# Projections of a pair of heads as one continuous stream over all pairs, shifted by half a period, with one PSUM pool of six banks

## The chip, the cores and the metric

The program runs on one core of one Trainium2 chip. The metric is device time in microseconds (us) for one execution. The engines are named as in the profile: PE (TensorE, matmuls and transposes; PEld are its weight loads), DVE (VectorE), ACT (ScalarE), POOL (GpSimd) and SP (SyncE, here the queue that issues nearly all DMAs). Each engine works through its own queue in order and waits on semaphores for the others.

## The reference, cut to what matters

The reference is a trunk of two layers on a sequence of 1024 positions of width 1024. The change touches only the token mixer of layer 0, the forgetting attention with 16 heads of width 64:

```python
def forgetting_attention(h, w_in, b_f, q_gain, k_gain, w_out):
    proj = h @ w_in                                   # [1024,1024] @ [1024, 4*1024+16]
    q, k, v, o, fl = jnp.split(proj, [D, 2 * D, 3 * D, 4 * D], axis=-1)
    q = rmsnorm(q.reshape(B, S, H, Dh), q_gain)
    k = rmsnorm(k.reshape(B, S, H, Dh), k_gain)
    F = jnp.cumsum(jax.nn.log_sigmoid(fl + b_f), axis=1).transpose(0, 2, 1)
    for qb in range(S // Q_BLOCK):                    # 8 blocks of 128 queries, causal
        logits = einsum('bqhd,bkhd->bhqk', q[:, q0:q1], k[:, :q1]) * Dh ** -0.5
        logits = where(kpos <= qpos, logits + F[:, :, q0:q1, None] - F[:, :, None, :q1], -inf)
        outs.append(einsum('bhqk,bkhd->bqhd', softmax(logits), v[:, :q1]))
    return (concatenate(outs) * sigmoid(o)) @ w_out
```

After it come `x + g1 * y`, a convolutional feed-forward, a spatial-gating layer with its own feed-forward, and a last norm. These later stages take the larger part of the time and the change leaves their code as it is.

## The kernel before, in words

Everything is computed in fp32 precision by splitting each operand into a high and a low part (`pair`: ACT casts the high part, DVE subtracts for the low part) and running three matmuls per product (`mm3`). All of the attention stands in one method, `fox`.

First come the norm of x, the modulation vectors and the gate o. The `o_proj` calls for the last five slices of o are mixed with `run_jobs`: each of its jobs reads 2 MB of `ada_w`, adds it up on DVE (`ada_part`, line 268) and ends in four tiny PE matmuls against a column of ones and one DVE add (line 283). The tiny matmuls, the transposes of q and k, and the transposes of the attention weights all use one PSUM pool of two banks, `ms`, whose users are chained in program order.

Then the heads are worked in eight pairs, p = 0 to 7. A pair needs:

- `proj(p)`: the columns of q, k and v for the pair, 8 blocks of 128 positions, each block 8 steps of three matmuls of 128x384 (192 matmuls named `pj<-x,h` in the profile). It is a generator that yields after each step, 64 steps in all. Its weights come by DMA through two `fraw` buffers and are split into eight `x` buffers (`weights`). After four blocks (a half) the norm of q and k runs on ACT and DVE, into one `qkv` buffer.
- `heads_qk(half)`: eight transposes (`ms<-ident,qkv`), from which ACT and DVE make the scaled high and low parts `qq`, `kh`, `kl`. `heads_v`: the same for v, without PE.
- `scores(qt)`, qt = 0 to 7: matmuls `s<-kh,qq` and `s<-kl,qq` for both heads, up to 512 keys a piece, a DVE pass that subtracts the bias built on POOL and takes the extremum (line 715), then the exponential and the scaling on ACT and DVE.
- `values(g, hd)`, g = 0 to 3: for each block of keys up to four transposes of the weights into an `ms` bank (`ms<-ident,cv` and `ms<-ident,raw`), the split into a `pt` buffer on ACT (line 750) and DVE (line 119), and matmuls with v, `pv<-pt,w`, issued one block later (`later`). At the end of a group the result is gated and written to DRAM (`nat`).

The projections of the next pair are the filler. `tick` takes as many steps from the generator `fill` as work was just issued: `n / P` for a piece of scores, 1 or 2 for a block of values. At the end of a pair `drain` takes what is left. For p = 7 the filler is `out_early`, the first part of the output projection (`pj<-h,h`, 128x512), whose operands come in pieces through the same two `fraw` buffers (`out_piece`); ahead of it `x_transposed` brings x and transposes it (64 transposes `ms<-ident,h`).

PSUM has eight banks: two for `ms`, three for `s` (pool `fs`), two for `pj` (pool `fpj`), one for `pv` (pool `fpv`).

The order on each engine is not the order of the source. A scheduler goes through the program with priorities in the order of the source and puts an instruction ahead when the ones before it are not ready and it has its buffers. With two banks of its own, `pj` can be taken ahead of the source at any place where PE would be without work.

Of the kernel before, what the change touches and what calls it, by code (L numbers as in the profile page):

```python
# [18 lines left out]
P = 128  # L19
# [48 lines left out]
class Trunk:  # L68


    def __init__(self, ctx, tc, **io):
        self.ctx, self.tc, self.nc = ctx, tc, tc.nc
        self.__dict__.update(io)
        self.chains = {}
        self.strict = self.ordered = False
        self.pending = None
        self.hooks = []
        self.ra, self.rx = "a", "X"
        self.n = 0
# [23 lines left out]
    def mm(self, out, lhsT, rhs, start, stop):  # L103
        i = self.nc.tensor.matmul(out, lhsT, rhs, start=start, stop=stop, skip_group_check=self.strict)  # L104
        return self.chain("pe", i) if self.strict else i
# [47 lines left out]
    def transpose4(self, srcs):  # L153

        ps = self.tile(self.ms, [P, 512], F32, "ms")
        for j, s in enumerate(srcs):
            i = self.nc.tensor.transpose(ps[: s.shape[1], j * P : (j + 1) * P], s, self.ident)  # L157
            if j == 0:
                self.chain("ms", i)
# [183 lines left out]
    def fox(self):  # L343
# [9 lines left out]
        with ExitStack() as es:  # L353
# [20 lines left out]
            def ps1(pool, tag):  # L374
                return pool.tile([P, 512], F32, tag=tag, name=self.name(tag))
# [22 lines left out]
            def raw_pieces():  # L398
# [7 lines left out]
                return [T([P, 2, 2, 256], F32, "pt", 2) for _ in range(2)]  # L406
# [65 lines left out]
            for p in range(3):  # L472
                for half in range(2):
                    acc[p, half] = ps1(*((ps_s, "s") if p == 0 else (ps_p, "pj")) if p < 2 else (ps_s, "s") if half else (ps_v, "pv"))
# [28 lines left out]
            def o_out(p, half, ps):  # L503
                t = T([P, 512], F32, "pt", 2)
# [7 lines left out]
            def o_proj(p):  # L512
                w = o_weights(3 * D + p * P)
                ps = [ps1(ps_s, "s"), ps1(ps_p, "pj")]
# [15 lines left out]
            def weights(p):  # L530
                ws = []
                n = 400 if p == 0 else 384
                for k0 in range(0, KT, 2):
                    raw = T([P, 2, 400], F32, "fraw", 2)
                    for t in range(3):
                        i = nc.sync.dma_start(
                            raw[:, :, t * P : (t + 1) * P],
                            w_in[k0 * P : (k0 + 2) * P, t * D + p * P : t * D + (p + 1) * P].rearrange(
                                "(k p) f -> p k f", p=P
                            ),  # L540
# [3 lines left out]
                    if p == 0:  # L544
                        nc.sync.dma_start(
                            raw[:, :, 384:], w_in[k0 * P : (k0 + 2) * P, 4 * D :].rearrange("(k p) f -> p k f", p=P)
                        )
                    for j in range(2):
                        t = self.xslot([P, 2, 400], F32R)
                        ws.append(self.pair(t[:, :, :n], raw[:, j, :n], "x"))  # L550
                return ws

            def proj(p, ws, rw):

                n = 400 if p == 0 else 384
                for half in range(2):
                    r = T([P, 4, 384], F32, "qkv", 3)
                    for s in range(4):
                        ps = ps1(ps_p, "pj")
# [60 lines left out]
            self.fill, self.due = iter(()), 0.0  # L620

            def tick(w):
                self.due += w
                while self.due >= 1:
                    self.due -= 1
                    next(self.fill, None)

            def drain():
                for _ in self.fill:
                    pass  # L630
                self.due = 0.0

# [29 lines left out]
            def heads_v(rw):  # L662
                v = self.wslot([P, NST, 256])
                for half in range(2):
                    vs = rw[half][:, :, 256:384].rearrange("p s (g d) -> p s g d", d=DH)
                    vd = v[:, 4 * half : 4 * half + 4, :].rearrange("p s (g d) -> p s g d", d=DH)
                    i = nc.scalar.copy(vd[:, :, 0:4:3, :], vs)
                    if half == 0:
                        self.chain("w", i)
                    self.split_lo(vd[:, :, 1:3, :], vs, vd[:, :, 0:4:3, :])  # L670
                return v
# [1111 lines left out]
```

## Time and profile before

| | us |
|---|---|
| median of three runs | 2730.57 (2730.3 to 2733.01) |
| the profiled execution | 2729.37 |
| its span | 2727.6 |
| PE busy (share of the span) | 2582.4 (95%) |
| DVE busy | 2092.0 (77%) |
| ACT busy | 1460.2 (54%) |
| POOL busy | 164.5 (6%) |
| first and last start of `s<-kh,qq` | 202.4 and 777.4 |
| first and last start of `pv<-pt,w` | 218.2 and 809.3 |

A row of busy time by stretch gives, for each engine, the microseconds in which it was busy and in brackets the number of instructions, then the mean granted clock of PE as a share of its full clock (PEclk), and the share and rate of the DMAs. A row of a timeline gives the start, the time to the end of the last instruction of the row, the engine, line, operation, what it writes and reads, and the count; idle time before it stands in square brackets with the instruction that ended it. Ends of matmuls are modelled and overlap, so the price of a matmul in a stream is read from one start to the next.

### The profile page before, as it was taken

Reading aid. Unit: us, or ns where it says so; the run is one execution under the profiler, and the core shown is the slowest. Engines: PE = TensorE matmul, PEld = TensorE weight load, DVE = VectorE, ACT = ScalarE, POOL = GpSimd, SP = SyncE. Lnnn points to the kernel's source line nnn. Section 1 sums busy time; section 2 is a strip of 40 time slices with the busy share of each in tenths; the row PEclk is TensorE's granted clock in tenths of the full one; section 3 lists DMA queues with packets and bytes.
Section 4 is the critical chain, followed back from the end, with each engine's and each line's share of the span. In section 5 each row is a group of like instructions: output and inputs, shape, how many; then the busy total and the mean of one; then the engine's idle time right before and its main releaser. Section 6 shows DMA issues by size and latency. Waiting matters only on the chain.

```text
span 2727.6 us, 35317 instructions
## 1 busy us (share of the span) xinstructions
PE 2582.4 (95%) x12522; PEld 2189.0 (80%) x12522; DVE 2092.0 (77%) x3630; ACT 1460.2 (54%) x2310; POOL 164.5 (6%) x289
## 2 busy tenths in 40 slices
PE   6999899998797899999999999999999999999997
PEld 5999888886685788888888878888877788888886
DVE  7467777678786888898688777666788888877875
ACT  7327666667654554454545654554456455545444
POOL 1012222223100000000000000000000000000000
PEclk8999999988897999999999999999999999999999
DMA  6572111131113144554846346557552343337562
GB/s 229 169 241 62 43 51 47 45 110 62 56 55 124 62 132 135 161 159 151 289 152 206 97 136 184 188 183 278 158 173 85 112 143 101 124 101 283 162 198 91
DMA packets 315512, 377.61 MB, mean 138 GB/s; under 512 B 18760, under 2 KB 196040, under 8 KB 315336
## 3 DMA queue, kind: packets, MB, share of 16 engines
q1 hardware_dynamic: 315112, 375.30, 42.1%
q8 instruction: 98, 1.61, 0.2%
q14 instruction: 78, 0.64, 0.1%
q10 hardware_dynamic: 224, 0.06, 0.0%
HBM read 285.57 MB, written 89.72 MB: 138 GB/s over the span
## 4 chain that ended last, share of the span: by engine, by line
PE 82%; DVE 10%; ACT 2%; issue 2%; DMA 2%; SPq 1%; POOL 0%; DVEq 0%; POOLq 0%; ACTq 0%
PE bankX L104 19%; PE banka L104 17%; PE bankY L104 17%; PE pj L104 14%; PE ms L104 5%; PE s L104 3%; PE ms L157 3%; PE pv L104 2%; DVE ow L994 1%; DVE hc L994 1%; DVE x L994 1%; PE ms L1600 1%; DVE x L1479 1%; DVE rw L994 1%; SPq L421 1%
## 5 line engine op out<-in xcount | busy, mean ns | idle before, releaser
L981 ACT CAST ow<-rw 128x1024 fp32r<-128x1024 f32 (+1 forms) x438 | 398.7, 911 | 474.6 <-PE bankX L104 156.3
L994 DVE TENSOR_TENSOR ow<-rw,ow 128x1024 fp32r<-128x1024 f32 (+1 forms) x438 | 457.7, 1046 | 171.9 <-ACT ow L981 171.4
L104 PE MATMUL bankX<-hc,ow 128*128 128x512 f32 x1920 | 470.3, 393 | 17.5 <-DVE ow L994 9.6
L104 PEld LDWEIGHTS bankX<-hc,ow 128*128 128x128 f32 x1920 | 361.0, 189 | 95.4 <-DVE ow L994 11.4
L104 PE MATMUL banka<-hc,ow 128*128 128x512 f32 x1608 | 393.4, 393 | 6.5 <-ACT hc L981 2.8
L104 PE MATMUL bankY<-hc,ow 128*128 128x512 f32 x1584 | 388.6, 392 | 0.8 <-DVE ow L994 0.8
L104 PEld LDWEIGHTS banka<-hc,ow 128*128 128x128 f32 x1608 | 301.1, 189 | 71.3 <-ACT hc L981 4.4
L104 PEld LDWEIGHTS bankY<-hc,ow 128*128 128x128 f32 x1584 | 296.5, 188 | 64.3 <-issue 1.9
L104 PE MATMUL pj<-x,h 128*128 128x384 f32 (+1 forms) x1536 | 302.0, 346 | 6.5 <-ACT qkv L566 6.5
L104 PEld LDWEIGHTS pj<-x,h 128*128 128x128 f32 x1536 | 272.8, 192 | 9.7 <-ACT qkv L566 7.5
L1479 DVE SCALAR_TENSOR_TENSOR x<-x,prm,x 128x1023 f32<-128x1023 f32 (+1 forms) x160 | 204.3, 1279 | 2.7 <-ACT x L1477 2.1
L104 PE MATMUL bankY<-ow 128*128 128x512 f32 x720 | 203.6, 391 | 0.2 <-DVE x L998 0.2
L104 PE MATMUL banka<-ow 128*128 128x512 f32 x672 | 187.3, 391 | 0.5 <-DVE x L998 0.5
L104 PEld LDWEIGHTS bankY<-ow 128*128 128x128 f32 x720 | 135.2, 188 | 28.5 <-DVE x L998 0.6
L104 PE MATMUL bankX<-ow 128*128 128x512 f32 x588 | 156.3, 392 | 0.0
L104 PEld LDWEIGHTS banka<-ow 128*128 128x128 f32 x672 | 125.8, 188 | 27.3 <-ACT x L1028 0.8
L104 PE MATMUL pv<-pt,w 128*128 128x256 f32 (+1 forms) x640 | 124.4, 309 | 18.6 <-DVE pt L119 10.1
L104 PE MATMUL ms<-ow 128*128 128x512 f32 x546 | 139.9, 390 | 0.9 <-DVE pp L994 0.9
L119 DVE TENSOR_TENSOR pt<-ms,pt 128x512 fp32r<-128x512 f32 (+1 forms) x160 | 100.1, 631 | 47.7 <-ACT pt L750 46.6
L104 PEld LDWEIGHTS pv<-pt,w 128*128 128x128 f32 x640 | 103.2, 208 | 33.5 <-DVE pt L119 16.4
L104 PEld LDWEIGHTS bankX<-ow 128*128 128x128 f32 x588 | 110.8, 188 | 23.9 <-issue 1.0
L104 PEld LDWEIGHTS ms<-ow 128*128 128x128 f32 x546 | 102.0, 188 | 23.7 <-DVE pp L994 2.9
(299 smaller groups left out, 3883.5 us busy)
## 6 DMA issues: line engine op xcount, KB each, us to landing
rw<-yd SPq DMA_DIRECT2D x210, 256.0 KB
rw<-in_ffn_w_up_dram SPq DMA_DIRECT2D x88, 512.0 KB
yd<-pp SPq DMA_DIRECT2D x60, 512.0 KB
rw<-in_ada_w_dram SPq DMA_DIRECT2D x48, 512.0 KB
rw<-in_ffn_w_down_dram SPq DMA_DIRECT2D x88, 256.0 KB
rw<-in_sgu_w_in_dram SPq DMA_DIRECT2D x32, 512.0 KB
yd<-x SPq DMA_DIRECT2D x30, 512.0 KB
fraw<-in_fox_w_in_dram SPq DMA_DIRECT2D x96, 128.0 KB
```

Source lines behind the costliest of these rows:

```text
L104: i = self.nc.tensor.matmul(out, lhsT, rhs, start=start, stop=stop, skip_group_check=self.strict)
L119: return (eng or self.nc.vector).tensor_tensor(lo, full, hi.bitcast(F32), op=ALU.subtract)
L157: i = self.nc.tensor.transpose(ps[: s.shape[1], j * P : (j + 1) * P], s, self.ident)
L421: i = nc.sync.dma_start(r[:, :, t, :], src[:, :, t, q * 256 : (q + 1) * 256])
L981: return self.ao(self.nc.scalar.copy(t[:, 0], src))
L994: return self.vo(self.nc.vector.tensor_tensor(out, a, b, op=op))
L1479: stt(o[:, j:], a[:, : S - j], w[2 - j], o[:, j:], op0=ALU.mult, op1=ALU.add)
L1600: k = nc.tensor.matmul(px[:, b * P : (b + 1) * P], vn[:, b, c * P : (c + 1) * P], sg[:, 0], start=True, stop=True)
```

## The change

The attention's projections become one generator over the pairs 1 to 7, `stream`, and not one per pair. It is no longer drained at the end of a pair: `tick` takes 0.85 of a step per unit of work, and `until` only makes sure that the half that is needed next is there. So the projections of pair p run from the middle of pair p - 1 to the beginning of pair p, half 0 before `heads_qk(rws[p], 0)` and half 1 after the first scores of pair p. The weights of the next pair are loaded and split inside the last block of a projection, buffer by buffer as its last readers are done. After the last projection the same stream does the transposes of x and `out_early`.

The three PSUM pools become one of six banks that `s`, `pv`, `pj`, `op` (the output projection) and `o` share. The matmuls with v run two blocks behind the transposes and not one, for which `pt` gets a third buffer. `bns`, a tile of a later stage, moves from one SBUF pool to another. The flag `inorder` is never set to true, so the chains that hang on it are not made.

```diff
-            ps_s = es_p.enter_context(tc.tile_pool(name="fs", bufs=3, space=PSUM, reuse_waits="tile"))
-            ps_p = es_p.enter_context(tc.tile_pool(name="fpj", bufs=2, space=PSUM, reuse_waits="tile"))
-            ps_v = es_p.enter_context(tc.tile_pool(name="fpv", bufs=1, space=PSUM, reuse_waits="tile"))
+            ps_f = es_p.enter_context(tc.tile_pool(name="fps", bufs=6, space=PSUM, reuse_waits="tile"))
...
+                load(0)
+                load(1)
+                yield
+                for j in range(4):
+                    for i in range(2):
                         t = self.xslot([P, 2, 400], F32R)
-                        ws.append(self.pair(t[:, :, :n], raw[:, j, :n], "x"))
-                return ws
+                        ws.append(self.pair(t[:, :, :n], raws[j][:, i, :n], "x"))
+                    if j < 2:
+                        load(j + 2)
+                    yield
...
-            def proj(p, ws, rw):
+            def proj(p, ws, rw, nw=None):
...
+                        if nw and half == 1 and s == 3:
+                            next(nw)
                         for k in range(KT):
+                            yield
                             self.mm3(
                                 ps[:, :n], [(h[half, k][0][:, ss], h[half, k][1][:, ss], *ws[k])], k == 0, k == KT - 1
                             )
-                            yield
+                            if nw and half == 1 and s == 3 and k % 2:
+                                next(nw)
...
             def tick(w):
-                self.due += w
+                self.due += w * self.rate
...
+            def until(p, half):
+
+                while len(rws[p]) <= half:
+                    next(self.fill)
...
+            def stream():
+
+                ws = []
+                nw = weights(1, ws)
+                for _ in nw:
+                    pass
+                for p in range(1, 8):
+                    ws2 = []
+                    nw = weights(p + 1, ws2) if p < 7 else None
+                    yield from proj(p, ws, rws[p], nw)
+                    ws = ws2
+                self.rate = 1.4
+                yield from x_transposed()
+                yield from out_early()
...
                     tick(1)
-                    if len(later) > 1:
+                    if len(later) > 2:
                         later.pop(0)()
-                        tick(1)
+                    tick(1)
...
+            self.fill = stream()
             fb = f_rows(0)
-            heads_qk(rw, 0)
-            heads_qk(rw, 1)
-            v = heads_v(rw)
+            heads_qk(rws[0], 0)
+            scores(0, fb, 0)
+            v0 = None
             for p in range(8):
...
+                if p:
+                    values(p - 1, 3, 1, v0)
+                v = self.wslot([P, NST, 256])
+                heads_v(rws[p], v, 0)
+                scores(p, fb, 1)
+                until(p, 1)
+                scores(p, fb, 2)
+                values(p, 0, 0, v)
+                scores(p, fb, 3)
+                heads_qk(rws[p], 1)
+                values(p, 0, 1, v)
+                heads_v(rws[p], v, 1)
...
+                scores(p, fb, 6)
                 if p < 7:
+                    until(p + 1, 0)
+                values(p, 2, 0, v)
+                scores(p, fb, 7)
+                values(p, 2, 1, v)
+                if p < 7:
                     fb = f_rows(p + 1)
-                    heads_qk(rw, 0)
-                    drain()
+                    heads_qk(rws[p + 1], 0)
                 values(p, 3, 0, v)
                 if p < 7:
-                    heads_qk(rw, 1)
                     scores(p + 1, fb, 0)
```

`x_transposed` becomes a generator too: it brings all eight blocks of x and the first pieces of `w_out` at once, yields eight times, and then yields after each of its sixteen groups of four transposes.

How this moves the queues is shown at three places; the names are those of the tiles, with the number of the tile behind each.

PE, the end of a pair's period in the middle of the stage (pair 4): pieces of the matmuls with v, the last transposes and the last scores. Before:

```order
L104 MATMUL pv_5672<-pt_5678,w_5346 128x256 x4
L104 MATMUL pv_5672<-pt_5712,w_5346 128x256 x2
L104 MATMUL pv_5672<-pt_5712,w_5346 128x128 x2
L157 MATMUL ms_5811<-ident,cv_5511 128x128
L157 MATMUL ms_5811<-ident,cv_5608 128x128
L157 MATMUL ms_5811<-ident,cv_5511 128x128
L157 MATMUL ms_5811<-ident,cv_5608 128x128
L157 MATMUL ms_5829<-ident,cv_5511 128x128
L157 MATMUL ms_5829<-ident,cv_5608 128x128 x2
L104 MATMUL s_5887<-kh_744,qq_743 128x512
L104 MATMUL s_5887<-kl_745,qq_743 128x512
L104 MATMUL pv_5799<-pt_5805,w_5346 128x256 x4
```

The same place now:

```order
L157 MATMUL ms_5796<-ident,cv_5488 128x128
L157 MATMUL ms_5796<-ident,cv_5578 128x128 x2
L104 MATMUL pv_5770<-pt_5776,w_5301 128x256 x3
L104 MATMUL pv_5770<-pt_5790,w_5301 128x256 x4
L104 MATMUL s_5855<-kh_738,qq_737 128x512
L104 MATMUL s_5855<-kl_739,qq_737 128x512
L104 MATMUL pj_5814<-x_5233,h_594 128x384 x3
L104 MATMUL pj_5814<-x_5254,h_620 128x384 x3
L157 MATMUL ms_5887<-ident,raw_5494 128x128
L157 MATMUL ms_5887<-ident,cv_5584 128x128
L157 MATMUL ms_5887<-ident,raw_5494 128x128
L157 MATMUL ms_5887<-ident,cv_5584 128x128
```

Before, each of the pairs 1 to 5 ends with 89 to 93 matmuls and transposes on PE among which no projection stands, and there are 223 in a row ahead of pair 7. Now no such run is longer than 40, but for one of 121 in pair 7, around the transposes of x.

PE, ahead of the first scores: the last tiny matmuls of the jobs (`ms<-ones,tm`) and the first transposes of q and k. Before, projections of pair 1 (`pj<-x,h`) stand between them:

```order
L277 MATMUL ms_1528<-ones,tm_1421 128x1 x4
L104 MATMUL pj_1866<-x_1702,h_570 128x384 x3
L104 MATMUL pj_1866<-x_1705,h_596 128x384 x3
L104 MATMUL pj_1866<-x_1712,h_622 128x384 x3
L104 MATMUL pj_1866<-x_1715,h_648 128x384 x3
L104 MATMUL pj_1952<-x_1682,h_409 128x384 x3
```

Now nothing stands between them, ahead of them is the last `o_proj`, and the first projection comes after the first scores:

```order
L104 MATMUL o_1568<-h_646,x_1564 128x512 x3
L279 MATMUL ms_1432<-ones,tm_1391 128x1 x4
L279 MATMUL ms_1522<-ones,tm_1415 128x1 x4
L279 MATMUL ms_1545<-ones,tm_1504 128x1 x4
L279 MATMUL ms_1551<-ones,tm_1528 128x1 x4
L157 MATMUL ms_1627<-ident,qkv_800 128x128 x4
L157 MATMUL ms_1636<-ident,qkv_800 128x128 x4
L104 MATMUL s_1659<-kh_738,qq_737 128x128
L104 MATMUL s_1659<-kl_739,qq_737 128x128
L104 MATMUL s_1660<-kh_738,qq_737 128x128
L104 MATMUL s_1692<-kh_738,qq_737 128x256
L104 MATMUL pj_1741<-x_1708,h_403 128x384 x3
```

150 matmuls of pair 1's projection have moved from ahead of the first scores to behind them.

SP, pair 0: the loads of the projection weights (`fraw`) beside the writes and reads of the groups of values (`nat`, `so`). Before, four loads stand together ahead of the pair's first `nat`:

```order
L536 DMA fraw_2568<-in_fox_w_in_dram 128x2x128 x3
L536 DMA fraw_2578<-in_fox_w_in_dram 128x2x128 x3
L536 DMA fraw_3445<-in_fox_w_in_dram 128x2x128 x3
L536 DMA fraw_3455<-in_fox_w_in_dram 128x2x128 x3
L771 DMA nat_95<-so_1828 128x256
```

Now they stand behind it, between the pair's third and fourth `nat`:

```order
L803 DMA nat_95<-so_2170 128x256
L770 DMA so_2691<-nso_96 128x256
L539 DMA fraw_2505<-in_fox_w_in_dram 128x2x128 x3
L539 DMA fraw_2529<-in_fox_w_in_dram 128x2x128 x3
L539 DMA fraw_3329<-in_fox_w_in_dram 128x2x128 x3
L539 DMA fraw_3333<-in_fox_w_in_dram 128x2x128 x3
L803 DMA nat_95<-so_2370 128x256
```

The loads have moved behind three writes of `nat`, which wait for DVE. The first two rows are chunks that the next projection needs; the last two are the first chunks of the projection after it.

More of the change, by code (lines that the diff above doesn't have):

```diff
@@ L405, in raw_pieces @@
                     return [self.wslot([P, 4, 2, 256], F32)]
-                return [T([P, 2, 2, 256], F32, "pt", 2) for _ in range(2)]
+                return [T([P, 2, 2, 256], F32, "pt", 3) for _ in range(2)]
             a, sh = (T([P, KT], F32, nm, 1) for nm in ("a01", "sh01"))
@@ L473, in fox @@
                 for half in range(2):
-                    acc[p, half] = ps1(*((ps_s, "s") if p == 0 else (ps_p, "pj")) if p < 2 else (ps_s, "s") if half else (ps_v, "pv"))
+                    acc[p, half] = ps1("o")
             done = [0, 0, 0]
@@ L528, in fox, with weights, load @@
             fq = T([P, P], F32, "fq", 1)
-            def weights(p):
-                ws = []
+            def weights(p, ws):
                 n = 400 if p == 0 else 384
-                for k0 in range(0, KT, 2):
-                    raw = T([P, 2, 400], F32, "fraw", 2)
+                raws = {}
+                def load(j):
+                    raw = raws[j] = T([P, 2, 400], F32, "fraw", 2)
+                    rows = slice(2 * j * P, (2 * j + 2) * P)
                     for t in range(3):
@@ L660, in flush, with heads_v @@
                     later.pop(0)()
[L662 to L671, printed above, removed]
+            def heads_v(rw, v, half):
+                vs = rw[half][:, :, 256:384].rearrange("p s (g d) -> p s g d", d=DH)
+                vd = v[:, 4 * half : 4 * half + 4, :].rearrange("p s (g d) -> p s g d", d=DH)
+                i = nc.scalar.copy(vd[:, :, 0:4:3, :], vs)
+                if half == 0:
+                    self.chain("w", i)
+                self.split_lo(vd[:, :, 1:3, :], vs, vd[:, :, 0:4:3, :])
             def f_rows(p):
@@ L708, in scores @@
                     n = c1 - c0
-                    pss = [ps1(ps_s, "s") for _ in range(2)]
+                    pss = [ps1("s") for _ in range(2)]
                     for hd in range(2):
@@ L781, in values @@
                     tick(1)
-                    if len(later) > 1:
+                    if len(later) > 2:
                         later.pop(0)()
-                        tick(1)
-            rw = []
-            self.fill = proj(0, weights(0), rw)
+                    tick(1)
+            ws = []
+            for _ in weights(0, ws):
+                pass
+            self.fill = proj(0, ws, rws[0])
             drain()
@@ L845, in x_transposed @@
                             self.chain("x", i)
+                        yield
+                    out_y(range(4), half)
+            self.inorder = False
+            self.fill = stream()
             fb = f_rows(0)
[L848 to L850 removed]
+            heads_qk(rws[0], 0)
+            scores(0, fb, 0)
+            v0 = None
             for p in range(8):
[L852 to L872 removed]
@@ new lines, in fox @@
+                if p:
[10 more added lines that the diff above has]
+                heads_v(rws[p], v, 1)
+                scores(p, fb, 4)
+                values(p, 1, 0, v)
@@ L880, in fox @@
                     scores(p + 1, fb, 0)
-                else:
-                    values(p, 3, 1, v)
+                v0 = v
+            values(7, 3, 1, v0)
             flush()
             drain()
+            self.inorder = False
             for i in range(2):
@@ L897, in fox @@
                         banks = Ring(self.bank["X"] + self.bank["Y"])
-                    for _ in out_mm(banks() if banks else ps1(ps_p, "pj"), range(PC, 8), m, half):
+                    for _ in out_mm(banks() if banks else ps1("op"), range(PC, 8), m, half):
                         pass
@@ L1553, in sgu @@
         gelu = AF.Gelu_apprx_tanh
[L1554 removed]
+        bns = self.ap.tile([P, NST, SG, 6], F32, name="bns")
         mv = self.const.tile([P, NST, 2], F32, name="bnm")
```

71 lines of the change are left out of this document (28 added, 43 removed).

## The prediction

> **What bounds the kernel now.** I read the page's slices first, then busy time by stretch through the attention, then the prices of PE's instructions, then its waits.
>
> ```profile
> PE   6999899998797899999999999999999999999997
> PEclk8999999988897999999999999999999999999999
> ```
>
> Each digit is a slice of 68 us. PE has work nearly everywhere, so a change must either take work from PE or fill its gaps, and this one takes no matmul away. The gaps lie in slices 5 to 11, the attention, and there the granted clock drops too. The stretches show how:
>
> ```profile
> core 0: us, PE busy (x) PEld busy (x) DVE busy (x) ACT busy (x) POOL busy (x), PEclk, DMA share, GB/s
> 250.00:260.00 10.00, 7.08 (x48) 6.70 (x47) 8.20 (x24) 7.53 (x15) 1.77 (x4) 1.00 0.01 2
> 260.00:312.00 52.00, 51.38 (x333) 49.95 (x331) 32.79 (x92) 31.86 (x72) 12.27 (x22) 1.00 0.17 46
> 312.00:336.00 24.00, 15.23 (x79) 12.89 (x79) 22.49 (x70) 17.86 (x31) 5.68 (x10) 0.84 0.15 56
> 336.00:385.00 49.00, 49.00 (x313) 48.38 (x312) 29.42 (x83) 27.98 (x64) 10.97 (x20) 0.98 0.16 44
> 385.00:411.00 26.00, 19.30 (x91) 15.50 (x90) 24.16 (x77) 18.45 (x32) 7.38 (x12) 0.74 0.19 61
> 411.00:462.00 51.00, 51.00 (x331) 50.13 (x329) 32.53 (x93) 32.89 (x74) 11.20 (x20) 1.00 0.16 45
> 462.00:486.00 24.00, 16.66 (x87) 13.35 (x86) 23.28 (x70) 17.75 (x32) 6.98 (x12) 0.84 0.18 61
> 536.00:561.00 25.00, 18.11 (x88) 14.49 (x86) 23.29 (x74) 17.50 (x30) 7.50 (x12) 0.73 0.19 64
> 612.00:637.00 25.00, 18.43 (x95) 15.09 (x94) 23.81 (x75) 19.01 (x34) 9.01 (x12) 0.83 0.17 59
> 652.00:735.00 83.00, 63.38 (x332) 50.42 (x330) 62.20 (x176) 60.28 (x121) 16.69 (x32) 0.88 0.14 48
> ```
>
> Dense stretches of some 50 us, in which PE is busy throughout, take turns with tails of some 25 us in which it is busy for 63 to 74%, has a granted clock of 0.73 to 0.84, and DVE is busy for 93 to 97%. A period (312 to 385 to 462) is 75 us. In a dense stretch DVE is busy for 60 to 64%. So the two engines are loaded by turns: DVE has 29.42 + 24.16 = 54 us of work in a 75 us period, and PE fills its share only while projections last. What a tail costs needs the price of PE's instructions in a stream, from one start to the next:
>
> ```profile
> 226.06 0.40 PE L104 MATMUL s<-kh,qq 128*128 128x512 f32 x1
> 226.29 0.39 PE L104 MATMUL s<-kl,qq 128*128 128x512 f32 x1
> 226.52 0.34 PE L104 MATMUL pj<-x,h 128*128 128x384 f32 x1
> 226.70 0.27 PE L157 MATMUL ms<-ident,cv 128*128 128x128 f32 x1
> 226.81 0.27 PE L157 MATMUL ms<-ident,raw 128*128 128x128 f32 x1
> ...
> 228.66 0.33 PE L104 MATMUL s<-kh,qq 128*128 128x384 f32 x1
> 228.83 0.34 PE L104 MATMUL s<-kl,qq 128*128 128x384 f32 x1
> ...
> 229.53 1.04 PE L104 MATMUL pv<-pt,w 128*128 128x256 f32 x8
> 230.41 0.29 PE L157 MATMUL ms<-ident,cv 128*128 128x128 f32 x1
> ...
> 232.96 3.14 PE L104 MATMUL pj<-x,h 128*128 128x384 f32 x17
> 235.94 0.39 PE L104 MATMUL s<-kh,qq 128*128 128x512 f32 x1
> ```
>
> A scores matmul of 512 columns takes 0.23 us, of 384 columns 0.17, a transpose 0.11, a matmul with v 0.88 / 8 = 0.11, a projection 2.98 / 17 = 0.175. The 89 instructions of one tail in the order (33 transposes, 40 matmuls with v, 12 scores of 512 and 4 of 384) come to 73 x 0.11 + 12 x 0.23 + 4 x 0.17 = 11.5 us, 0.13 us each. The five tails (312, 385, 462, 536 and 612) hold 79 + 91 + 87 + 88 + 95 = 440 of them, 57.2 us of work at that price, and last 124 us. **A tail loses 66.8 / 5 = 13.4 us.** What PE waits for there is DVE, in small pieces:
>
> ```profile
> PE s L104 <- DVE smx L715: 15.5, 11, 2.8
> PE pv L104 <- DVE pt L119: 10.1, 18, 1.5
> PE ms L157 <- DVE pt L119: 7.1, 11, 1.8
> ```
>
> **The change part by part.** *The tails.* The order shows that projections now stand between the last scores and the values of a pair, where none stood. All 192 matmuls of a projection are still made. The five tails, of pairs 1 to 5, give 66.8 us back if nothing else is late. Pair 0's end loses less, since projections reach into it: 2.9 us idle in 250 to 260 and 0.6 behind it. The stretch ahead of pair 7 loses more:
>
> ```profile
> L104 PE MATMUL pj<-h,h 128*128 128x512 f32 x46 | 13.4, 432 | 0.2 <-ACT h L126 0.2
> L157 PE MATMUL ms<-ident,h 128*128 128x128 f32 x64 | 9.5, 292 | 6.8 <-ACT x L843 2.8 <-issue 2.7 <-DVE kl L649 1.3
> ```
>
> Of its 332 instructions, 46 are output projections of 512 columns, 0.23 us each, and 286 are of the tail's kind, 0.13 each: 47.8 us of work in 83, **35 us lost**. Together 66.8 + 3.5 + 35 = 105 us can be won at most in this stage. It is the sum of all losses there, not a forecast.
>
> *What is late next in each pair.* A period without its loss is 75 - 13.4 = 62 us of PE work. DVE's 54 us would fill 87% of that, so PE stays the bound, but closely. That both can run at once is shown where output projections stand evenly between pair 7's steps:
>
> ```profile
> 750.00:780.00 30.00, 30.00 (x166) 25.85 (x165) 28.30 (x78) 20.19 (x38) 6.47 (x10) 1.00 0.26 86
> ```
>
> PE has no gap in 30 us while DVE is busy for 28.3. This is the lower bound, 0 lost per pair; the tail's 13.4 is the upper one. I take a value by the nearest rows. Pair 0's end, a pair boundary with filler near it, lost 2.9 + 0.6. The hand-over of weights comes on top: chunks 3 and 4 of the next weights can be loaded only when chunks 1 and 2 are split, and ACT stands still for them:
>
> ```profile
>   DMA fraw<-in_fox_w_in_dram: 2.6, 3
> ```
>
> That is 2.6 us over two pairs, 1.3 each (0 to 2.6). The loads now queue on SP behind the third `nat` write, which waits for DVE; behind them stand the next `so` reads, needed only at a group's end. The hand-over has eleven steps of projection between chunk 1's split and the first reader of chunk 3, 33 x 0.175 = 5.8 us, with the pair's other PE work among them, and that is its cover; without it PE would wait those microseconds. **4.8 us per pair, 34 us over seven pairs.** The one pool of six banks adds a wait: a bank is handed on only when its last reader is done, and a `pv` bank is held through a whole group. Behind a waiting matmul stands all of PE, and DVE's score pass waits for it. The row on `smx` above, 15.5 us at three banks, is what such a wait cost; six shared banks can cost less or as much, and it lies within the 13.4 already.
>
> *The start.* This is a new wait. The jobs on `ada_w` end late, and before, PE worked on pair 1's projection meanwhile:
>
> ```profile
> 170.78 0.84 PE L104 MATMUL pj<-h,x 128*128 128x512 f32 x3
> 171.46 1.22 PE L104 MATMUL pj<-x,h 128*128 128x384 f32 x6
> ...
> 185.75 7.20 PE L104 MATMUL pj<-x,h 128*128 128x384 f32 x40
> 192.79 0.95 PE L277 MATMUL ms<-ones,tm 128*128 128x1 f32 x8
> ...
> 202.44 0.22 PE L104 MATMUL s<-kh,qq 128*128 128x128 f32 x1
> ```
>
> ```profile
> 186.27 3.32 DVE L268 SCALAR_TENSOR_TENSOR tm<-cv,cact,tm 128x512 f32<-128x512 f32 x4 [0.17 <-DMA cv<-in_ada_w_dram]
> ```
>
> The last `o_proj` matmul is issued by 171.5. DVE ends the last job at 186.27 + 3.32 = 189.6. In the new order PE stands at `ms_1432` to `ms_1551` until then, with eight transposes, the scores and all projections behind it; DVE's adds to `mod` and ACT's first `qq` wait for them. After that the first scores need `heads_qk` on ACT:
>
> ```profile
> L647 ACT ACTIVATE kh<-ms,prm 64x512 fp32r<-64x512 f32 x32 | 21.7, 678 | 4.6 <-PE ms L157 4.0 <-DVE kl L649 0.3
> L653 ACT CAST kh<-kh 64x512 fp32r<-64x512 f32 x32 | 19.8, 618 | 0.7
> ```
>
> Two `qq` and two `kh` at 0.68 and two casts at 0.62 us are 4 us, and with the transposes the first projection starts at about 195. In those 23.5 us PE has 4 x 0.95 + 8 x 0.11 = 4.7 us of its own work (the tiny matmuls of four jobs and the transposes), so it loses **19 us, and 1 at a low clock: 20**. Nothing else covers it; the SP queue is the same up to there, so the jobs come no earlier. Bounds: 15, if the jobs end when their last load lands, and 24, if the scores wait for one more of DVE.
>
> *The end.* Pair 7 now has the transposes of x, and then output projections, as filler; their operands come through the same two `fraw` buffers, so ACT waits as before:
>
> ```profile
> L126 ACT CAST h<-fraw 128x512 fp32r<-128x512 f32 x15 | 9.2, 618 | 5.3 <-DMA fraw<-nat 3.3 <-DMA fraw<-in_fox_w_out_dram 1.8
> ```
>
> Of the 35 us, 13 belong to the tail of pair 6 and 22 to this. The 64 transposes of x (7 us) now fill part of it, and 121 instructions in a row are still without a projection: **15 us**, between 10 and 22.
>
> *The rest.* A third `pt` buffer and the place of `bns` cost nothing: no instruction is added. Matmuls with v two blocks late give DVE's split one block more of time; the row `pv <- pt` above (10.1 us) is inside the tails. The rows from the last output projection on are the same in both orders.
>
> **Sum:** 105 - 34 - 20 - 15 = 36 us won. The profiled execution takes 2729.4 (span 2727.6), so 2693.4; the median of the runs is 1.2 us above it, which gives **2694.6**.
>
> **Rivals.** *All fills up*: 1 us per pair, start 19, end 10: 36 us left of 105, 69 won, **2661.6**. For it: the stretch at 750. Against: there the filler has 0.23 us matmuls and no norm of q and k.
>
> *The stalls move inside*: PE works in order, and a projection between two dependent steps helps only if the step behind it is ready. If each pair keeps its 13.4 us, 7 x 13.4 + 20 + 15 = 129 are lost in place of 105, **24 us slower, 2754.6**. It decides from (105 - 35) / 7 = 10 us per pair on. For it: DVE at 93 to 97% in the tails. Against: its 60 to 64% ahead of them.
>
> *The clock*: the mean of the tails' granted clock is 0.80; were that full speed and half speed by turns, 25 us x 0.2 x 2 = 10 us of a tail would be at half speed and, with PE busy for some 70% of it, cost 3.5 us. If the remaining small waits keep it so low for as long in every pair, 7 x 3.5 = 25 us are added to the forecast: **2719.6**. Against it stands the row 250 to 260, with 2.9 us idle at 1.00. The Trainium skill, TensorE: Matmul & The Clock Gate, section "A second HAM failure mode: psum-queue depth-cycling", describes this: PE idling briefly but often between groups of matmuls, while banks are cycled, makes the clock swing between half and full. The same page's section "Why this matters for your kernels" warns only of a single gap of over about 3 us; the longest wait quoted above, 2.8 us, is shorter and the clock drops all the same, so the trace bears out the first section more. By the second alone each tail would have lost 3.5 us less.
>
> *It doesn't do what it says*: the scheduler could have taken the projections ahead as before; the order speaks against it. It would leave the time at 2730.6.
>
> **Chances.** The forecast (2677 to 2713) 0.54, all fills up 0.20, the clock 0.10, no change 0.05, stalls inside 0.11. A measurement can tell about 0.2%, 5.5 us, from no change. Faster: 0.54 + 0.20 + 0.10 = 0.84; same 0.05; slower 0.11. The range 2656 to 2738 takes in the bounds per pair, start and end but not the full price of the stalls.
>
> **What would show it.** Right: no tails in the busy time by stretch, PE above 90% and DVE about 80% from 200 to 740, a period of 67 us; PE idle and below full clock between 172 and 195; the last matmul with v 30 to 36 us earlier. Wrong: a period of 72 us or more with DVE no busier; waits of PE for `fraw` or `x`; or PE kept busy between 172 and 195 after all.

## The result, and the profile after

The changed kernel takes **2735.66 us** in the median (2733.7 to 2738.74), against 2730.57 before: a ratio of 1.0019 (1.0011 to 1.0027), 5 us slower. The forecast was 2694.6 (2677 to 2713). The wider range of 2656 to 2738 holds the measured time, but only because it leaves room for losses that the forecast did not expect. The profiled execution takes 2735.38, its span is 2733.6.

The slices of the page, as in the prediction, 68 us each:

```profile
PE   6978998998897899999999999999999999999997
PEclk9989999999998999999999999999999999999999
```

The third slice has a new gap, 7 where a 9 stood. From the fifth to the eleventh the 8s and 9s are spread otherwise, but not gone; none of these slices is as empty as the eleventh was. The waits of PE between 171 and 832 us (total, times, longest):

```profile
PE ms L157 <- DVE qq L684: 24.3, 13, 3.2
PE pv L104 <- ACT pt L782: 17.3, 16, 2.2
PE ms L279 <- DVE tm L270: 14.4, 3, 5.5
PE ms L157 <- DVE kl L684: 6.7, 6, 1.7
```

The waits for `smx` and for DVE's `pt` that carried the prediction are gone from the top of the list (for DVE's `pt` 2.2 us are left). In their place PE waits for a bank of `ms` that DVE has still to read for `qq` and `kl`, and for ACT's half of `pt`. `ms <- tm` is the new gap at the start.

Busy time by stretch, cut where pairs begin (every 48th scores matmul), first before, then after:

```profile
262.50:339.60 77.10, 67.71 (x411) 63.95 (x410) 54.99 (x160) 49.01 (x100) 17.96 (x32) 0.93 0.16 50
339.60:414.80 75.20, 68.50 (x408) 64.11 (x407) 55.52 (x160) 49.08 (x100) 18.35 (x32) 0.91 0.16 48
```

```profile
171.00:195.70 24.70, 8.15 (x41) 7.58 (x39) 18.69 (x31) 3.73 (x8) 8.63 (x14) 0.55 0.65 233
...
256.60:331.60 75.00, 67.31 (x414) 64.26 (x413) 55.69 (x161) 50.10 (x101) 17.59 (x30) 0.93 0.18 52
331.60:405.00 73.40, 66.37 (x410) 63.40 (x409) 56.84 (x161) 49.86 (x100) 20.48 (x32) 0.94 0.16 50
...
479.60:552.80 73.20, 66.25 (x417) 63.21 (x416) 57.18 (x163) 50.84 (x102) 18.44 (x32) 0.97 0.17 51
```

Each of the pairs 1 to 5 takes 73 to 75 us, where it took 75 to 77. What a stretch loses can be read from its row: the time in which PE is not busy, and of its busy time the share by which its clock falls short. Pair 1 after: 75.0 - 67.3 = 7.7, and 0.07 x 67.3 = 4.7. Worked out in this way, but with the exact stretches of half clock in the trace, the losses are (one profiled execution of each kernel; "pairs" is 0 to 7, from the first scores to the last, "rest" from there to the next stage):

| kernel | median us | start (from 171) | pairs | of these 1 to 5, mean | rest |
|---|---|---|---|---|---|
| before | 2730.57 | 0 | 94.3 | 12.4 | 0 |
| changed | 2735.66 | 20.2 | 88.7 | 10.7 | 0 |
| changed, three old pools (e3) | 2723.36 | 0 | 89.2 | 10.1 | 0 |
| before, pool of six (e5) | 2754.44 | 18.0 | 104.8 | 14.9 | 2.3 |
| products one block late, not two (e8) | 2746.88 | 19.4 | 105.5 | 13.1 | 0 |
| fill behind heads_qk (e1) | 2732.7 | 18.2 | 85.2 | 11.8 | 0.4 |
| q and k in the pool (e4) | 2710.87 | 2.7 | 76.4 | 8.6 | 0.8 |
| early first half (e2) | 2710.2 | 2.7 | 70.7 | 8.3 | 2.6 |
| low parts on POOL (e6) | 2738.53 | 18.3 | 91.1 | 10.7 | 0 |
| e2 and e4 together (e7) | **2689.58** | 0.6 | 56.2 | 5.0 | 2.9 |
| e7, lead used up (e10) | 2693.83 | 0.6 | 61.7 | 7.8 | 0.2 |
| rate 0.80 (e12) | 2733.3 | 18.9 | 85.1 | 9.0 | 0 |
| rate 0.92 (e13) | 2708.37 | 18.5 | 61.0 | 7.5 | 2.2 |
| e7 at rate 0.92 (e14) | 2691.26 | 0.6 | 63.7 | 5.4 | 3.5 |

PE's work in this stage, what is left when the losses are taken off, comes to 555 to 566 us in all of them, so the table is good to some 5 to 8 us between kernels, and what differs by less it does not decide. From before to after the losses rise by 14.6 and the time by 5 to 6; the difference of 8 to 9 lies at the edge of that.

By this table the change won 6 us in the pairs and lost 20 at the start.

### The profile page after: what moved, and what is told of

It reads as the page before. It is cut to its first block, busy times and chain, and to the rows that moved or that the text cites. A ratio compares the mean times of both kernels' runs of the same rounds, so it can differ in the third digit from the quotient of the medians.

```text
span 2733.6 us, 35259 instructions
## 1 busy us (share of the span) xinstructions
PE 2572.6 (94%) x12522; PEld 2186.8 (80%) x12522; DVE 2100.1 (77%) x3630; ACT 1464.2 (54%) x2310; POOL 164.1 (6%) x289
## 4 chain that ended last, share of the span: by engine, by line
PE 80%; DVE 10%; ACT 4%; DMA 3%; issue 3%; SPq 0%; POOL 0%; DVEq 0%; ACTq 0%; POOLq 0%
PE bankX L104 20%; PE banka L104 18%; PE bankY L104 17%; PE pj L104 8%; PE ms L104 5%; PE op L104 3%; PE ms L157 3%; PE s L104 2%; PE pv L104 2%; DVE hc L1037 1%; DMA fraw<-in_fox_w_in_dram 1%; DVE ow L1037 1%; PE ms L1643 1%; DVE x L1037 1%; PE o L104 1%
## 5 line engine op out<-in xcount | busy, mean ns | idle before, releaser
L104 PE MATMUL bankX<-hc,ow 128*128 128x512 f32 x1920 | 470.0, 393 | 17.5 <-DVE ow L1037 9.6
L104 PE MATMUL pj<-x,h 128*128 128x384 f32 (+1 forms) x1536 | 317.5, 352 | 0.1
L104 PEld LDWEIGHTS pj<-x,h 128*128 128x128 f32 x1536 | 279.8, 197 | 3.9 <-DVE smx L747 0.3
L104 PE MATMUL pv<-pt,w 128*128 128x256 f32 (+1 forms) x640 | 121.9, 295 | 18.5 <-ACT pt L782 17.3
L782 ACT CAST pt<-ms 128x512 fp32r<-128x512 f32 (+1 forms) x160 | 85.3, 540 | 74.2 <-PE ms L157 71.0
```

The source lines that it names most:

```text
L782: nc.scalar.copy(pt[:, 0, :nb], ps[:, :nb])
```

## The experiments

**Which part makes the start gap: the pool or the new order?** Two kernels make a two by two table with before and after. In e3 the changed kernel has the old pools:

```diff
-            ps_f = es_p.enter_context(tc.tile_pool(name="fps", bufs=6, ...))
+            ps_s, ps_p, ps_v = ...   # bufs 3, 2, 1
```

> The changed kernel with the three PSUM pools of before (three banks for s, two for pj and op, one for pv) in place of the one of six; the accumulators of o are placed as before. Theory A (waits of heads_qk): 2730 to 2745, no faster than the changed kernel, the wait of ms for qq stays at some 24 us and one of s for smx comes back. Theory B (the shared pool ties s, pj and pv together and makes the idle time): 2700 to 2720.

Measured: 2723.36, ratio to before 0.9978 (0.9969 to 0.9987). In e5 the kernel before has the pool of six and nothing else.

> The kernel before with nothing changed but the PSUM pools: one of six banks that s, pv, pj and o share, in place of three, two and one. With the kernel before, the changed one and the changed one with the old pools this makes a two by two table. Theory P (the shared pool hands banks on in program order, so that projections can't be taken ahead of the first scores, and it helps a little inside the pairs): the start loses some 20 us as in the changed kernel, the pairs win 0 to 10: 2735 to 2755. Rival (the start gap comes from the new program order of the stream and not from the pool): no idle time between 171 and 200, 2715 to 2735.

Measured: 2754.44, ratio 1.0084 (1.007 to 1.0097). The first stretch, from the last `o_proj` to the first scores, in e3 and in e5:

```profile
171.00:201.50 30.50, 30.50 (x191) 30.47 (x191) 18.60 (x31) 8.91 (x16) 9.72 (x14) 1.00 0.46 164
```

```profile
171.00:193.50 22.50, 8.14 (x41) 7.57 (x39) 17.13 (x29) 3.71 (x8) 9.06 (x14) 0.55 0.63 227
```

```profile
180.70 1.84 PE L277 MATMUL ms<-ones,tm 128*128 128x1 f32 x8 [3.96 <-DVE tm L268]
187.75 1.83 PE L277 MATMUL ms<-ones,tm 128*128 128x1 f32 x8 [5.22 <-DVE tm L268]
```

With the old pools PE has no gap there (1.00, 191 matmuls), with the pool of six it is busy for 8 of 22 us even in the code before. **The gap comes from the pool**: its banks are handed on in the order of the program, and a projection cannot take one ahead of the first scores. The pool costs 24 us in the code before and 12 in the changed one; the rest of the change, without it, wins 7. For e3 both theories missed: the time lies between their ranges, and the waits are not those of theory A. That for `qq` falls from 24.3 to 6.7 us, and others take its place, so that the loss in the pairs is the same, 89:

```profile
PE ms L157 <- DVE pt L119: 13.1, 17, 2.2
PE pj L104 <- ACT qkv L583: 13.1, 8, 2.5
PE ms L157 <- DVE qq L688: 6.7, 4, 2.5
```

In e5 theory P had the total and the start right, but not the pairs: they were to win 0 to 10 us and lose 10.5 more, 104.8. Yet on PE e5 has the order that the forecast counted on: in the pairs 0 to 6 of its trace no run of more than 40 instructions without a projection is left. In e3, runs of 48 to 56 come back in four of the pairs 1 to 5. **So the pool takes the tails out of the order even without the stream, and an order without tails did not by itself make the pairs faster.**

**Is the longer distance of the products worth something?** In e8 they are one block late again.

```diff
-                    if len(later) > 2:
+                    if len(later) > 1:
```

> The changed kernel with the matmuls with v one block behind the transposes, as before, and not two; the third pt buffer stays. If the longer distance pays as forecast (0 to 10 us in the wait of pv for pt): slower than the changed kernel by 3 to 20 us, 2738 to 2755, with pv waiting for pt for more than 17 us. If it pays nothing: within 3 us of it.

Measured: 2746.88, 1.0063 (1.005 to 1.0075), as expected if the distance pays. The second block is worth 11 us, although the wait of `pv` for ACT's `pt` is only 2.8 us longer without it. The wait for `qq` grows too, by 8.3 us to 32.6, and of the 17 us that the table shows in the pairs, 10 are time lost at half clock:

```profile
PE pv L104 <- ACT pt L782: 20.1, 14, 2.6
```

**What holds PE up in the pairs?** The timeline of the changed kernel at the end of pair 1, on PE, and on ACT in the same 6 us:

```profile
321.86 0.60 PE L157 MATMUL ms<-ident,qkv 128*128 128x128 f32 x4
...
323.40 0.60 PE L157 MATMUL ms<-ident,qkv 128*128 128x128 f32 x4
323.76 0.53 PE L104 MATMUL pv<-pt,w 128*128 128x256 f32 x3
327.49 0.45 PE L157 MATMUL ms<-ident,raw 128*128 128x128 f32 x1 [3.20 <-DVE qq L684]
...
329.52 0.45 PE L157 MATMUL ms<-ident,raw 128*128 128x128 f32 x1 [0.95 <-DVE kl L684]
```

```profile
322.49 0.68 ACT L682 ACTIVATE qq<-ms,qg 64x512 fp32r<-64x512 f32 x1 [0.32 <-PE ms L157]
323.48 0.48 ACT L579 COPY qkv<-pj 128x384 f32<-128x384 f32 x1 [0.31 <-PE pj L104]
324.04 0.68 ACT L682 ACTIVATE kh<-ms,prm 64x512 fp32r<-64x512 f32 x1
324.75 0.36 ACT L798 COPY av<-pv 64x256 f32<-64x256 f32 x1
325.02 0.61 ACT L688 CAST kh<-kh 64x512 fp32r<-64x512 f32 x1
325.66 0.68 ACT L682 ACTIVATE qq<-ms,qg 64x512 fp32r<-64x512 f32 x1
326.37 1.15 ACT L758 ACTIVATE cv<-cv,smx 128x1024 f32<-128x1024 f32 x1
...
327.63 0.68 ACT L682 ACTIVATE kh<-ms,prm 64x512 fp32r<-64x512 f32 x1
```

The eight transposes of q and k take both banks of `ms`. ACT makes the four scaled parts one by one, with a copy of a projection, a gated result, a cast and an exponential between them, and DVE follows. The next transposes of weights wait for 3.20 and 0.95 us, and the projections stand behind them. All waits of this kind come to the 24.3 + 6.7 us shown above.

Before, the same transposes were followed by projections:

```profile
330.44 0.65 PE L157 MATMUL ms<-ident,qkv 128*128 128x128 f32 x4 [1.76 <-DVE pt L119]
330.85 0.54 PE L104 MATMUL pv<-pt,w 128*128 128x256 f32 x3
332.78 6.64 PE L104 MATMUL pj<-x,h 128*128 128x384 f32 x22 [1.39 <-ACT qkv L566]
```

The source has these 22 only in the next pair; the scheduler took them ahead through the two banks of `pj`. At 321 us PE had done 528 projection matmuls of the pairs from 1 on in the kernel before (192 are a pair), 528 in e3, 384 in e5 and 357 in the changed kernel. So the old pools let the projections run up to three quarters of a pair ahead of the source, and the one pool takes this lead away. In e5, the code before with that pool, no projection is left to stand there, and the wait for `qq`, 1.5 us in all before, becomes the longest of all:

```profile
326.12 0.66 PE L157 MATMUL ms<-ident,qkv 128*128 128x128 f32 x4 [2.60 <-DVE pt L119]
...
330.90 1.08 PE L157 MATMUL ms<-ident,cv 128*128 128x128 f32 x4 [3.83 <-DVE qq L648]
```

```profile
PE ms L157 <- DVE qq L648: 52.1, 13, 8.1
```

This wait, then, like the gap at the start, appears with the one pool. A second place lies at the beginning of each pair:

```profile
265.64 0.27 PE L157 MATMUL ms<-ident,raw 128*128 128x128 f32 x1
268.16 0.39 PE L104 MATMUL pv<-pt,w 128*128 128x256 f32 x1 [2.25 <-ACT pt L782]
```

```profile
263.90 0.93 ACT L126 CAST x<-fraw 128x384 fp32r<-128x384 f32 x2 [1.28 <-DMA fraw<-in_fox_w_in_dram]
264.73 0.47 ACT L579 COPY qkv<-pj 128x384 f32<-128x384 f32 x1
265.24 1.06 ACT L585 ACTIVATE cv<-qkv 128x1024 f32<-128x1024 f32 x1
266.20 0.60 ACT L700 CAST w<-qkv 128x512 fp32r<-128x512 f32 x1
266.71 0.92 ACT L126 CAST x<-fraw 128x384 fp32r<-128x384 f32 x2
267.53 0.58 ACT L782 CAST pt<-ms 128x512 fp32r<-128x512 f32 x1
```

ACT has six passes of weights, projection, norm and v to make ahead of the `pt` for which PE stands 2.25 us. Three edits test this. e1 puts eight steps of the stream behind the transposes of q and k, and lowers the rate of `tick` to 0.75; e4 gives these transposes banks of the pool:

```diff
                     heads_qk(rws[p + 1], 0)
+                    for _ in range(8):
+                        next(self.fill)
```

> The changed kernel with eight steps of the stream (24 projection matmuls, 4.2 us) between the first half's heads_qk of the next pair and the last values of this one; the tick rate is lowered from 0.85 to 0.75 so that a pair still takes about 64 steps. Theory A: the gain went into a new wait there: the eight transposes of q and k hold both ms banks until DVE has made qq and kl, the transposes of the attention weights stand right behind them on PE, and the projections, which could cover it, behind those (24.3 + 6.7 us of PE waiting for qq and kl in 200 to 740, and 3.4 to 6.8 us of half clock after each). Then that wait falls below 8 us and the time by 15 to 35 us, to 2700 to 2720. Theory B, that the six shared banks or the hand-over of the weights hold the matmuls up: the same time within 5 us, and the idle time turns up in front of s or pj. Theory C, that only the start costs: the same time.

```diff
-                    ps = self.transpose4([rw[half][:, s, t * P : (t + 1) * P] for s in range(4)])
+                    ps = ps1("qk")
+                    for s in range(4):
+                        nc.tensor.transpose(ps[:, s * P : (s + 1) * P], rw[half][:, s, t * P : (t + 1) * P], self.ident)
```

> The changed kernel with the transposes of q and k in two banks of the six-bank pool, in place of the two ms banks; nothing else is changed. Theory A: the transposes of the attention weights no longer stand behind qq and kl; the wait of ms for qq and kl (31 us in 200 to 740) falls below 5 us and the time by 10 to 30 us, to 2705 to 2725; a part may come back as a wait of s for kh or of any matmul for a bank of the pool. Theory B (the shared pool is too small): slower, 2740 or more.

Measured: e1 2732.7, 1.0012 (1.0003 to 1.0021), 3 us below the changed kernel; e4 2710.87, 0.9925 (0.9913 to 0.9938), 25 below. Waits of e1, then of e4:

```profile
PE pv L104 <- ACT pt L782: 21.5, 16, 4.0
PE ms L157 <- DVE qq L684: 17.5, 7, 5.5
...
PE s L104 <- DVE qq L684: 5.4, 3, 2.1
```

```profile
PE pv L104 <- ACT pt L784: 17.1, 15, 2.2
PE ms L157 <- DVE pt L119: 12.1, 15, 2.6
...
PE s L104 <- DVE qq L686: 7.5, 10, 2.7
```

Theory A's 2700 to 2720 was missed by e1: the waits for `qq` and `kl` did not fall below 8 us, only from 31.0 to 20.5, and those for `pt` and of the scores grew; of the 10.5 us, 3 reached the time. So what the whole wait is worth e1 does not tell, but a part of it was worth little. In e4 the wait is gone and the time is in theory A's range, though in good part by luck: by the table only 12 us of the gain are in the pairs (88.7 to 76.4), and 17.5 are at the start: the transposes of q and k no longer stand behind the tiny `ms` matmuls of the jobs, so the first scores come at 175.7 and not at 195.7. That was not foreseen. (The edit calls the transposes directly and so leaves out, with the banks, the chain that `transpose4` puts on the users of `ms`; which of the two counts at the start was not separated.)

e6 takes DVE work away:

```diff
-                        ws.append(self.pair(t[:, :, :n], raws[j][:, i, :n], "x"))
+                        ws.append(self.pair(t[:, :, :n], raws[j][:, i, :n], "x", lo_eng="gpsimd" if p else "vector"))
```

> The changed kernel with the low parts of the projection weights of pairs 1 to 7 subtracted on POOL in place of DVE: 8 subtractions of 128x384 a pair, 0.5 us each on DVE, so some 4 us of DVE work a pair less, and perhaps 8 to 9 us of POOL work more. Theory D (what PE waits for in a pair is DVE and ACT being behind in bunches where the norm, the heads and the split of weights come together): the loss per pair falls from 11 to 7 to 9 us, the time by 10 to 30, 2705 to 2725. Theory A (only the two ms banks held by q and k count): at most 5 us faster. A rival on the other side: POOL delivers late, PE waits for x or for the score bias, slower than the changed kernel by 5 us or more.

Measured: 2738.53, 1.0035 (1.0021 to 1.0048). After and e6, 200 to 626 us:

```profile
200.00:626.00 426.00, 384.74 (x2383) 367.38 (x2382) 325.55 (x930) 291.16 (x586) 108.07 (x184) 0.95 0.17 51
```

```profile
200.00:626.00 426.00, 385.18 (x2389) 366.95 (x2387) 308.09 (x887) 290.07 (x586) 149.26 (x229) 0.95 0.16 50
```

DVE has 17 us less to do and PE is busy for the same 385; no wait of PE for POOL appears. **DVE's amount of work is not what bounds the pairs**; theory D is refuted in this form.

**Does the position of the stream matter?** e2 makes the first half of pair 1's projection ahead of the first scores:

```diff
             self.fill = stream()
+            for _ in range(32):
+                next(self.fill)
             fb = f_rows(0)
```

> The changed kernel with 32 steps of the stream (the first half of pair 1's projection, 96 matmuls) in the program ahead of the first heads_qk, so that they stand between the last tiny matmuls of the ada_w jobs again. All theories: PE's 17 us of idle time and the 27 us at half clock between 171 and 212 are gone, 17 to 24 us of the start; the first scores begin at about the same 196. The stream runs 32 steps ahead of the changed kernel from then on, so it ends sooner: if the freed 17 us of PE work are worth it at the end, 2712 to 2720; if the later pairs are bound by their waits and not by PE's work, little is won, 2725 to 2735.

Measured: 2710.2, 0.9923 (0.991 to 0.9935). That is a little better than the better of the two ranges. By the table 17.5 us come from the start and 18 from the pairs, where the stream now is 32 steps ahead, and 2.6 are lost again in the rest. That is 33, and the time fell by 25: here the table is 7 off. Both edits together:

> The changed kernel with both edits that won: the first half of pair 1's projection ahead of the first scores, and the transposes of q and k in two banks of the six-bank pool. If the two cure different losses: both won 25 us against the changed kernel, of which the start's part (17 and some 11 to 17) is common, so the sum is 30 to 38 us below it, 2697 to 2706. If the later loss is set by something else (the bunches on DVE and ACT): no better than either, 2705 to 2712.

Measured: 2689.58, 0.985 (0.9837 to 0.9864), better than expected and the fastest of all. A stretch of pair 4 shows what the forecast had hoped for:

```profile
467.80:534.10 66.30, 63.91 (x419) 61.16 (x418) 56.60 (x163) 50.74 (x102) 16.96 (x30) 1.00 0.19 57
```

66 us, PE busy for 96%, DVE for 85%, full clock. e10 keeps both edits and uses the lead up in pair 0, by a rate of 0.43 there:

> The kernel with both winning edits (first half of pair 1's projection ahead of the first scores, q and k transposed into banks of the six-bank pool), but with the tick rate at 0.43 while pair 0 is worked and 0.85 from pair 1 on, so that the stream's lead of 32 steps is used up in pair 0: at the boundaries of pairs 2 to 7 PE's order then has made about as many projection matmuls as in the changed kernel (522, 715, 906, 1098 and 1296 against 516, 713, 898, 1095 and 1293; with both edits and no lower rate 600, 816, 1006, 1200 and 1392). The start is cured either way. Theory F (the lead itself helps in the pairs, since the norm and the split of a half are then made well ahead of the heads that need it): the loss of pairs 1 to 5 rises from 5.0 on average to 7.5 to 9.5, as in the kernel with the qk banks alone, and pair 0, with half the filler, loses more: 2698 to 2712. Theory G (the lead does nothing but fill the start): within 4 us of the kernel with both edits, 2685 to 2694.

Measured: 2693.83, 0.9867 (0.985 to 0.9883). By the total it is theory G, by the places theory F: pairs 1 to 5 lose 7.8 and not 5.0 each, and pairs 6 and 7 lose 10.0 where e7 loses 17.9. The stream lasts longer in e10 (its last projection starts at 663.8 us, that of e7 at 644.0); that this is the reason was not tested. The last three runs change only the rate, of the changed kernel (0.80, 0.92) and of e7 (0.92):

> The changed kernel with a tick rate of 0.80 in place of 0.85: the projections stand a little thinner, and until makes up the rest in a row where a half is needed. It asks how much of the loss hangs on how evenly the filler is spread. Theory H (the stalls stand at fixed places of the program, where two matmuls in a row depend on each other through ACT and DVE, and filler spread by the amount of work doesn't meet them): within 8 us of the changed kernel, 2728 to 2744, and the loss per pair stays at 10 to 12. Rival (too little filler between the steps is what is wrong): clearly slower, 2745 or more.

> The same with 0.92: the stream runs ahead slowly, some 5 steps a pair, and ends half a pair sooner. Theory H: within 8 us of the changed kernel, 2728 to 2744. Rival (denser filler and a growing lead cure the stalls): 2710 to 2725.

> The kernel with both winning edits (early first half, q and k in banks of the pool) at a tick rate of 0.92 in place of 0.85. Theory H: within 8 us of it, 2682 to 2698. Rival (denser filler helps further in the pairs, less is left for the end): 2670 to 2682; or the stream is used up too soon and pairs 6 and 7 lose more than the others win: 2698 or more.

Measured: 2733.3, 1.001 (1.0001 to 1.002); **2708.37**, 0.992 (0.9908 to 0.9933); 2691.26, 0.9852 (0.9839 to 0.9866). A rate of 0.92 alone, with the start gap still there, wins 27 us over the changed kernel: the rival of theory H holds for e13, by more than its range. Pairs 1 to 5 lose 7.5 us each, and pair 7 loses 0.8 in place of 12.4, since the transposes of x (661 to 694 us) now stand in pair 6. On top of e7 it wins nothing. A thinner stream changes the time little. So a lead of the stream over the half that is needed next goes with 2.4 to 3.2 us less loss a pair (e2 and e13 against the changed kernel, e7 against e10). This is not proof: e12, without a lead, also loses 1.7 less a pair than the changed kernel (9.0), and e3, whose projections run far ahead, loses 10.1. Nor is it shown through which of the passes on ACT and DVE a lead would help; the wait of `pv` for ACT's `pt` is 17.3 us in the changed kernel, 12.9 in e13 and 10.4 in e7, but 9.6 in e10, whose lead is used up.

## Why the prediction was wrong

- **The 105 us** that could be won at most were too many: by the trace 94.3. The tails were priced at 0.13 us an instruction; with the time at half clock counted directly, pairs 1 to 5 lost 12.4 each and not 13.4, pair 6 and pair 7's stretch 29.6 and not 35.
- **"4.8 us per pair, 34 us over seven pairs" is the step that failed.** Pairs 0 to 6 lose 76.3 us, 10.9 each; the 42 us more are as much as the whole miss of 41. Pair 0's end and the stretch at 750 were taken as the nearest rows, and the hand-over of weights as the only new thing. What came in its place are waits for which the sum had no term: 31 us for `qq` and `kl` behind the transposes of q and k, and 17.3 for ACT's `pt`. The forecast read the order for runs without a projection, and not for which instruction stands directly behind a slow hand-over; where that waits, the projections wait as well. The wait for `qq` is large only with the one pool (1.5 us before, 6.7 in e3, 52.1 in e5). But it is not the whole cause: with little or none of it the pairs 1 to 5 still lose 10.1 us each in e3 and 8.6 in e4, by other waits. What sets that remaining loss stays open.
- **The one pool of PSUM banks** had no price of its own: its waits were to lie "within the 13.4 already". It costs 24 us in the code before and 12 here, and without it the change would have been 7 us faster than the kernel before (e3).
- **The rival "the stalls move inside"** had 0.11 and is what happened. Its point of decision, 10 us per pair, was on the right side: 10.9 were measured, and the kernel is slower. (With the measured 94.3, start and end it would be (94.3 - 32.6) / 7 = 8.8.) Its time, 2754.6, was too high, because it took 13.4 per pair where 10.9 were lost.
- **The start, 20 us (15 to 24)**: measured 20.2. The size was right, and the order was read rightly; but the prediction put the gap down to the new program order, and what makes that order is the shared pool (e3, e5). The prediction saw in the pool only a wait within the pairs.
- **The end, 15 us (10 to 22)**: pair 7 loses 12.4, within the bounds.
- **"A third pt buffer costs nothing" and the products two blocks late**: without the second block of distance the kernel is 11 us slower (e8), so the part pays more than was said.
- **The clock rival** asked whether half clock would stay: it does. The pairs lose 28.9 us to it, and lost 33.6 before. By itself it would have given 2719.6; it came on top of the idle time.
- **What would show it wrong** had a period of 72 us or more with DVE no busier: it is 74, with DVE busy for 76% (325.55 of 426) against 74% (325.85 of 439 in 202 to 641 before).

```profile
202.00:641.00 439.00, 398.45 (x2406) 375.79 (x2405) 325.85 (x948) 289.44 (x592) 108.46 (x184) 0.93 0.19 60
```

What stays open besides: why e10 and e4, with the stream at nearly the same places, differ by 13 us in pairs 6 and 7, and what the last 5 us per pair of e7 are.

## What to carry to other kernels

Filler that is spread evenly by amount of work does not by itself fill stalls that stand at fixed places: look in the order at what stands directly behind each slow hand-over of a bank, and give that hand-over other banks than the instructions behind it need (e4). Before pools are merged, ask which work was running ahead through banks of its own; here that was worth 24 us in the old code and 12 in the new. Do not judge such a stream by a single rate: 0.92 in place of 0.85 turned 5 us lost into 22 won, though on top of e7 it won nothing.

## What the runs showed of the hardware

The granted clock of PE steps between 1 and one half, at multiples of 3.41 us. I cut the stretch from 175 to 825 us of all fourteen profiled executions into such windows. Of full-speed windows in which PE was busy for less than 40%, 100 of 100 were followed by half speed; between 40 and 60%, 57 of 106; above, 1 of 2157. From half speed it came back after 148 of 152 windows that were busy for 90% or more, 12 of 37 at 80 to 90%, and none of 108 below. Of those 57 windows 55 touch no idle stretch of more than 3 us. So no single long wait is needed, and once down, PE must be busy for almost a whole window: at half clock its work takes longer and it looks busier than it is. Around and behind the waits of 3.20 and 0.95 us shown above:

```profile
327.30:334.10 6.80, 5.66 (x22) 5.32 (x23) 4.53 (x14) 4.72 (x13) 0.00 (x0) 0.50 0.11 39
```

The prediction weighed two sections of the Trainium skill, TensorE: Matmul & The Clock Gate: "A second HAM failure mode: psum-queue depth-cycling" and "Why this matters for your kernels". The first says that brief idle moments between groups of matmuls make the clock swing, the second warns of a single gap of more than about 3 us. The runs bear out the first: 57 of 106 windows that were busy for 40 to 60% brought the clock down, 55 of them without an idle stretch of more than 3 us.
